# Dilated attention in pairs of blocks, a pair every 24 bulk matmuls, beside the projections of a hybrid decoder layer

## The chip, the cores and the metric

One core of a Trainium2 chip runs the whole program in one launch. The metric is the device time of one execution in microseconds. The kernel before took 2669.09 us (median of 3 runs, 2668.16 to 2672.79).

The engines have names in the profile: PE is TensorE (matmuls and transposes), PEld its weight loads, DVE is VectorE, ACT is ScalarE, POOL is GpSimd, SP is the engine whose queue issues the DMAs. Each engine works through its own list of instructions in a fixed order and waits on semaphores for the others.

## The reference, cut to what matters

One decoder layer for 1024 tokens of width 1024, in float32: a SwiGLU, then a mixer with two branches, then a second SwiGLU, and a last norm. The mixer multiplies the normed tokens by one wide matrix `w_in`. Its first columns give the queries, keys and values of branch A, which is causal attention with dilation: 12 heads of 64 in three groups (dilation 1, 4 and 16). A group regroups the sequence by residue, and a block of 128 queries sees its own block of keys and, in the first two groups, the block before it.

```
s = einsum('brnqhd,brnkhd->brnhqk', qb, kw) * Dh**-0.5
s = where(valid, s, -inf);  m = max(s);  p = exp(s - m);  l = sum(p)
o = einsum('brnhqk,brnkhd->brnqhd', p / l, vw);  lse = m + log(l)
```

The three groups are mixed by a softmax over `lse`. The other columns of `w_in` feed branch B, a gated DeltaNet of 8 heads (short convolution, l2 norm, a triangular solve in every chunk, a scan over the chunks), and the merge gates. `merged @ w_out` is added to the residual.

## The kernel before

The program has a first SwiGLU (to about 750 us), the mixer (to about 1790 us) and the second SwiGLU with the last norm.

In the mixer the projections with `w_in` are the bulk of PE's work: each output tile of 128 x 512 is 24 matmuls in `proj` (line 229: 8 slices of the contraction, three products each, since a float32 operand is split into a high and a low part, H and L). `values` has a shorter bulk matmul for the first group (line 634). Into this stream the class `Weave` puts all the rest. It counts modelled time: `fill` adds 0.23 for a bulk matmul and, when `stretch` has gone by since the last look, polls a heap of tasks (generators) that are due; each polled task records its next few instructions and yields. PE's order is exactly the order of recording (`keep_in_program_order`); on DVE, ACT and SP a list scheduler orders by priority bands (`att` ahead of `h0` ... `h7` ahead of `bulk`) when operands are modelled to be ready.

During attention the stretch is `WIDE`, 2.76, which is 12 bulk matmuls of 0.23; when the last block is done it becomes `STRETCH`, 2.07. I call the instructions of one poll a slot. `attention` (line 789) advances every block that is going by one step in each slot, oldest first, then starts one new block. There are 48 blocks: 3 groups x 2 pairs of heads (`hp`) x 8 blocks. A block needs 256 keys (its own and the block before) or 128. For its two heads, in four slots:

- the scores QK, `tC<-ka` (line 747), one bank of PSUM for each head; head 0 lies in partitions 0 to 63 of the queries and keys, head 1 in 64 to 127. DVE adds the mask and takes the maximum (749), makes `nm` (752), ACT takes the exponential (754);
- an empty step;
- the transposes of the probabilities, `tM<-ident,s` (763), which ACT and DVE copy to `pT` (768, 766);
- the product with the values AV, `tA<-ka,pT` (775); ACT copies it to `o` (777), and a DMA on SP's queue writes `o` to the tensor `od` of the group (786).

So a slot in the middle holds AV of one block, the transposes of a later one, and QK of a third. A float32 matmul that is no transpose appears as two MATMUL records in the profile, a transpose and a bulk matmul (fp32r) as one.

Behind attention come the heads of branch B. For head 0, while attention still runs: the convolutions (927), `products` (L1017 on PE, evicted by DVE at 1019), the blockwise inverse, whose input goes through memory (`nbd`, 1075, and back into the tile `U`, 1079) and which is a chain of small DVE steps (1088, 1089); and turns of 128 x 128 tiles (934), which share the two banks `tA` with AV and the products. Buffers: `ka` has 11 slots of 128 x 1024, `sc` six of 128 x 256, `o` four.

Of the kernel before, what the change touches and what calls it, by code (L numbers as in the profile page):

```python
# [21 lines left out]
NT = T // P  # L22
EPS = 1e-6
NEG = -1.0e30
# [65 lines left out]
def psum(C, tag):  # L90
    return C.pp.tile([P, 512], F32, name=tag, tag=tag, bufs=BANKS[tag])


@contextmanager
def band(C, name):

    saved = C.tc.cur_priority
    C.tc.cur_priority = C.bands[name]
    yield
    C.bands[name] = C.tc.cur_priority  # L100
    C.tc.cur_priority = saved

WIDE, STRETCH = 2.76, 2.07


class Weave:
# [11 lines left out]
    def pe(self, ins, us):  # L120

        self.tc.keep_in_program_order(ins)
        self.now += us
# [24 lines left out]
def in_band(C, name, task):  # L148

    while True:  # L150
        with band(C, name):
            delay = next(task, None)
        if delay is None:
            return
        yield delay
# [6 lines left out]
def t4(C, tag, dt=F32):  # L162
    return C.mx.tile([P, T + {"U": 32, "xp": 16}.get(tag, 0)], dt, name=tag, tag=tag, bufs=TILES[tag])
# [169 lines left out]
def seven_weights(C, w, c0, rest=False):  # L333
# [7 lines left out]
    f1, f2 = raws  # L341
    S = C.fp.tile([P, 4, 4, P], F32, name="wS", tag="wS", bufs=1)
    S1, S2, S3, S4 = [S[:, i] for i in range(4)]
    for out, p, q, op in ((S1, f2[:, 0:4], f2[:, 4:8], ALU.add), (S2, S1, f1[:, 0:4], ALU.subtract),
                          (S3, f1[:, 0:4], f2[:, 0:4], ALU.subtract), (S4, f1[:, 4:8], S2, ALU.subtract)):
        nc.gpsimd.tensor_tensor(out=out, in0=p, in1=q, op=op)  # L346
    W = {}
    for srcs, names, eng in ((f1, (1, 2), nc.vector), (S[:, 0:2].rearrange("p a k n -> p (a k) n"), (5, 6), nc.vector),
                             (S[:, 2:4].rearrange("p a k n -> p (a k) n"), (7, 3), nc.vector), (f2[:, 4:8], (4,), nc.vector)):
        if rest and 1 in names:  # L350
# [291 lines left out]
def decay_cols(C, I):  # L642

    nc = C.nc
    n = NT * HEADS
# [1 line left out]
    def col(name, dt=F32):  # L647
        return C.mx.tile([P, NT, HEADS], dt, name=name)

    pool = t4(C, "g")  # L650
    used = [0]

    def tmp(name, n=NT * HEADS):
        used[0] += n
        v = pool[:, used[0] - n:used[0]]
        return v.rearrange("p (c h) -> p c h", h=HEADS) if name else v
# [7 lines left out]
    e, w, t, u, g = tmp("de"), tmp("dw"), tmp("dt"), tmp("du"), tmp("dg")  # L664
# [32 lines left out]
    ps = psum(C, "tA")  # L697
# [31 lines left out]
    return out  # L729


def attention_block(C, q, k, g, hp, V, b):

    nc = C.nc
    pe = C.weave.pe
    prev = (g == 0 and b > 0) or (g == 1 and b % 2 == 1)
    nk = 256 if prev else P
    mask = C.pair if g == 2 else (C.band if prev else C.band[:, P:])
    k0 = (b - prev) * P
    with band(C, "att"):  # L740
        o = C.mx.tile([P, 132], F32, name="o", tag="o", bufs=4)
        nm = C.mx.tile([P, 2], F32, name="nm", tag="nm", bufs=4)
        S = []
        for h in range(2):
            rows = slice(h * 64, h * 64 + 64)
            ps = psum(C, "tC")
            pe(nc.tensor.matmul(ps[:, :nk], q[rows, b * P:b * P + P], k[rows, k0:k0 + nk], start=True, stop=True), nk * 0.0017)
            s = C.mx.tile([P, 256], F32, name="s", tag="sc", bufs=6)
            nc.vector.tensor_tensor_reduce(s[:, :nk], ps[:, :nk], mask, 1.0, NEG, op0=ALU.add, op1=ALU.max,
                                           accum_out=o[:, 128 + h:129 + h])  # L750
            S.append(s)
        nc.vector.tensor_scalar(nm, o[:, 128:130], -0.125, None, op0=ALU.mult)
        for h in range(2):
            nc.scalar.activation(S[h][:, :nk], S[h][:, :nk], AF.Exp, bias=nm[:, h:h + 1], scale=0.125,
                                 accum_out=o[:, 130 + h:131 + h])
    yield
    yield
    with band(C, "att"):
        pTs = []
        for h in range(2):  # L760
            pt = psum(C, "tM")
            for j in range(nk // P):
                pe(nc.tensor.transpose(pt[:, j * P:j * P + P], S[h][:, j * P:j * P + P], C.ident), 0.11)
            pT = C.mx.tile([P, 256], F32, name="pT", tag="sc", bufs=6)
            if h % 2:
                nc.vector.tensor_copy(pT[:, :nk], pt[:, :nk])
            else:
                nc.scalar.copy(pT[:, :nk], pt[:, :nk])
            pTs.append(pT)
    yield  # L770
    with band(C, "att"):
        po = psum(C, "tA")
        for h in range(2):
            for j in range(nk // P):
                pe(nc.tensor.matmul(po[:, h * 64:h * 64 + 64], pTs[h][:, j * P:j * P + P],  # L775
                                    V[b - prev + j][hp][:, h * 64:h * 64 + 64], start=j == 0, stop=j == nk // P - 1), 0.19)
        nc.scalar.copy(o[:, :P], po[:, :P])
        dst = C.od[g][:, hp, :]
        if g == 0:
            dst = dst[b * P:b * P + P, :]  # L780
        elif g == 1:
            r, n = b // 2, b % 2
            dst = dst.rearrange("(i r) f -> r i f", r=4)[r, n * P:n * P + P, :]
        else:
            dst = dst.rearrange("(i r) f -> r i f", r=8)[b]
        nc.sync.dma_start(dst, o)


def attention(C):

    going = []
    while C.blocks or going or C.more:
        going = [b for b in going if next(b, True) is None]
        if C.blocks and C.blocks[0][0] <= C.weave.now:
            b = C.blocks.pop(0)[1]
            next(b)
            going.append(b)
        yield C.weave.stretch
    C.attended = True
    C.weave.stretch = STRETCH  # L800
# [511 lines left out]
def mixer(C, tc, I):  # L1312

    nc = C.nc
# [5 lines left out]
    gates = [(C_GA + f * P, C.sgad[f]) for f in range(8)] + [(C_GB + f * P, C.sgbd[f]) for f in range(8)]  # L1320

    with tc.tile_pool(name="mx", bufs=1) as C.mx:
        C.logit = C.mx.tile([P, NT, 16], F32, name="logit")
        with band(C, "att"):
            gdn_consts(C, I)
            rope = [t4(C, tag)[:, :T] for tag in ("U", "Tm")]
# [5 lines left out]
        for g in range(3):  # L1332
            V = values(C, I, w_in, g) if g else None
            for hp in range(2):
                q, k = [rope_tile(C, w_in, c0 + g * 256 + hp * P, g) for c0 in (C_QA, C_KA)]
                if V is None:
                    V = values(C, I, w_in, g)
                    for task in (decay_cols, conv_weights):
                        C.weave.add(in_band(C, "att", task(C, I)), 0.5)
                for b in range(NT):  # L1340
                    C.blocks.append((C.weave.now + 10.0, attention_block(C, q, k, g, hp, V, b)))
                    if g == hp == b == 0:
                        C.weave.add(attention(C), 0.0)
        C.heads, C.more, C.segs, C.combining = [], False, False, False
# [30 lines left out]
        while work or gates or last:  # L1375
            if work and free(*work[0]):
                what, h = work.pop(0)
# [265 lines left out]
```

## Time and profile before

| | |
|---|---|
| profiled execution, its own time | 2673.94 us |
| its span, first to last instruction | 2672.2 us |
| median of 3 timed runs | 2669.09 us |
| PE matmul busy | 2581.1 us, 97% of the span |
| DVE, ACT, POOL busy | 55%, 39%, 18% |
| granted TensorE clock, mean | 0.99 |
| first QK starts, last AV starts | 784.58 us, about 1057 us |

Read it so: PE has work in hand nearly all the time, so what it spends per instruction and what it waits for is the time of the kernel. The other engines count where PE waits for them. The stretch that the change touches is 784 to 1057 us, and the beginning of the heads behind it.

### The profile page before, as it was taken

The page shows a single profiled execution, that of the slowest core. Times are in us where ns is not written, and L with a number is a line of the kernel's source. Part 1 is how long each engine was busy: PE and PEld are TensorE (multiplying, and loading weights), DVE is VectorE, ACT ScalarE, POOL GpSimd, SP SyncE. Part 2 cuts the span into 40 slices and gives each one's busy share as a digit, 9 for nine tenths or more (in the row PEclk, how much of TensorE's full clock was granted, in tenths as well). Part 3 has the DMA queues.
Part 4 walks back from the last instruction along what each step waited for, and adds up shares of the span by engine and source line. Part 5 has one row for each costly group of instructions (what it writes and reads, how often), then busy time and mean ns, then how long its engine had stood idle before and what let it go on. Part 6 is the DMA issues. An engine that isn't in the chain of part 4 may idle for free. (4 is left out here: it accounts for less than half of the span.)

```text
span 2672.2 us, 34694 instructions
## 1 busy us (share of the span) xinstructions
PE 2581.1 (97%) x13007; PEld 2138.7 (80%) x13007; DVE 1463.4 (55%) x3276; ACT 1032.2 (39%) x1738; POOL 468.3 (18%) x378
## 2 busy tenths in 40 slices
PE   6999999999999999999999999999999999999997
PEld 5888888788788788787788888877877888887886
DVE  6444444432743547868867878445764444444326
ACT  5333333211544338445454444344433333332113
POOL 5534442000200000000000000000004445430002
PEclk9999999999999999999999999999999999999999
DMA  5323223531331222223222222367533232226311
GB/s 151 90 88 89 81 76 97 199 101 58 112 99 51 74 74 55 62 68 90 78 62 62 60 59 72 121 204 241 182 99 104 79 90 87 80 83 216 102 57 71
DMA packets 298809, 262.12 MB, mean 98 GB/s; under 512 B 39856, under 2 KB 232592, under 8 KB 298640
## 3 DMA queue, kind: packets, MB, share of 16 engines
q1 hardware_dynamic: 298640, 259.90, 31.9%
q8 instruction: 102, 1.67, 0.3%
q14 instruction: 67, 0.55, 0.1%
HBM read 195.26 MB, written 58.29 MB: 95 GB/s over the span
## 5 line engine op out<-in xcount | busy, mean ns | idle before, releaser
L229 PE MATMUL mm<-hH,wL 128*128 128x512 f32 x1072 | 442.0, 412 | 0.1
L229 PE MATMUL mm<-hL,wH 128*128 128x512 f32 x1072 | 419.8, 392 | 0.0
L229 PE MATMUL mm<-hH,wH 128*128 128x512 f32 x1072 | 418.9, 391 | 0.0
L204 ACT CAST wH<-wraw 128x1024 fp32r<-128x1024 f32 (+1 forms) x138 | 143.7, 1045 | 300.8 <-PE mm L537 123.8
L229 PEld LDWEIGHTS mm<-hL,wH 128*128 128x128 f32 x1072 | 201.5, 188 | 45.7
L229 PEld LDWEIGHTS mm<-hH,wL 128*128 128x128 f32 x1072 | 202.2, 189 | 43.7 <-issue 5.3
L205 DVE TENSOR_TENSOR wL<-wraw,wH 128x1024 fp32r<-128x1024 f32 (+1 forms) x138 | 169.7, 1231 | 112.8 <-ACT wH L204 105.6
L229 PEld LDWEIGHTS mm<-hH,wH 128*128 128x128 f32 x1072 | 202.5, 189 | 35.1
L355 DVE TENSOR_TENSOR wL<-wS,wH 128x1024 fp32r<-128x1024 f32 x88 | 126.8, 1441 | 162.1 <-ACT wH L354 161.3
L346 POOL TENSOR_TENSOR wS<-wraw 128x512 f32<-128x512 f32 x66 | 84.1, 1295 | 563.9 <-PE tA L296 322.8
L423 POOL TENSOR_TENSOR su<-su,sg 128x512 f32<-128x512 f32 x84 | 133.3, 1598 | 185.8 <-DVE su L397 161.6
L354 ACT CAST wH<-wS 128x1024 fp32r<-128x1024 f32 x88 | 92.5, 1053 | 151.0 <-PE tC L365 110.0
L393 ACT COPY ev<-mm 128x512 f32<-128x512 f32 (+1 forms) x118 | 68.5, 581 | 201.7 <-PE mm L365 201.7
L537 PE MATMUL mm<-wH,hidH 128*128 128x512 f32 x352 | 137.8, 392 | 3.0 <-DVE x L539 1.9
L537 PE MATMUL mm<-wH,hidL 128*128 128x512 f32 x352 | 137.5, 391 | 2.6 <-DVE hidL L205 2.6
L537 PE MATMUL tC<-wH,hidH 128*128 128x512 f32 x352 | 137.4, 391 | 1.9 <-ACT wH L204 1.9
L537 PE MATMUL mm<-wL,hidH 128*128 128x512 f32 x352 | 137.1, 390 | 1.3 <-DVE wL L205 1.3
L537 PE MATMUL tC<-wL,hidH 128*128 128x512 f32 x352 | 137.6, 391 | 0.5 <-DVE wL L205 0.5
L537 PE MATMUL tC<-wH,hidL 128*128 128x512 f32 x352 | 137.7, 391 | 0.0
L914 POOL MEMSET xp<- 128x3 f32 x24 | 2.4, 100 | 653.9 <-PE tA L775 250.9
L539 DVE SCALAR_TENSOR_TENSOR x<-mm,x 128x512 f32<-128x512 f32 x64 | 44.0, 689 | 105.2 <-PE mm L537 104.3
L539 DVE SCALAR_TENSOR_TENSOR x<-tC,x 128x512 f32<-128x512 f32 x64 | 44.0, 688 | 86.6 <-PE tC L537 86.5
(432 smaller groups left out, 6029.0 us busy)
## 6 DMA issues: line engine op xcount, KB each, us to landing
wraw<-in_w_in_dram SPq DMA_DIRECT2D x64, 512.0 KB, 4.1
wraw<-in_ffn_w_gate_dram SPq DMA_DIRECT2D x48, 512.0 KB, 4.6
hd<-su SPq DMA_DIRECT2D x84, 256.0 KB, 3.2
wraw<-in_ffn_w_down_dram SPq DMA_DIRECT2D x33, 512.0 KB, 4.3
wraw<-hd SPq DMA_DIRECT2D x33, 512.0 KB, 4.7
wraw<-in_ffn_w_up_dram SPq DMA_DIRECT2D x26, 512.0 KB, 4.7
xs<-in_ffn_w_up_dram SPq DMA_DIRECT2D x22, 512.0 KB, 3.9
wraw<-in_w_branch_b_dram SPq DMA_DIRECT2D x16, 512.0 KB, 4.5
```

The source lines that it names most:

```text
L204: nc.scalar.copy(H[:, :width], raw[:, :width])
L205: (nc.gpsimd if C.pool_split else nc.vector).tensor_tensor(out=L[:, :width], in0=raw[:, :width], in1=H[:, :width].bitcast(F32), op=ALU.sub ...
L229: ins = nc.tensor.matmul(ps, w[:, k, :], x[:, k, :], start=k == 0 and i == 0, stop=k == kt - 1 and i == 2)
L346: nc.gpsimd.tensor_tensor(out=out, in0=p, in1=q, op=op)
L354: nc.scalar.copy(H[:, :n], srcs)
L355: eng.tensor_tensor(out=L[:, :n], in0=srcs, in1=H[:, :n].bitcast(F32), op=ALU.subtract)
L393: nc.scalar.copy(v[:, s], ps[:, s])
L423: (eng or C.nc.gpsimd).tensor_tensor(out=out, in0=out, in1=sg, op=ALU.mult)
L537: nc.tensor.matmul(ps, h[:, m], w, start=i == 0, stop=i == len(seq) - 1)
L539: nc.vector.scalar_tensor_tensor(xs, ps, 0.5, xs, op0=ALU.mult, op1=ALU.add)
L914: nc.gpsimd.memset(xp[:, 0:3], 0.0)
```

## The change

`WIDE` becomes 5.52, so a slot comes every 24 bulk matmuls. A task is now a pair of neighbouring blocks, and each of its three steps does both blocks: QK of both (per head, both blocks into one bank at columns 0 and 256), then the transposes of both in the next slot (the empty step is gone), then AV of both into one bank with one copy on ACT. The scores of a pair lie in one `ka` slot; `o` holds two blocks and has three buffers. The logits of the decay move from a tile of their own into the tile `g`.

```
-WIDE, STRETCH = 2.76, 2.07
+WIDE, STRETCH = 5.52, 2.07
...
-def attention_block(C, q, k, g, hp, V, b):
+def attention_pair(C, q, k, g, hp, V, b0):
...
+        o2 = C.mx.tile([P, 2, 132], F32, name="o", tag="o", bufs=3)
+        nm = C.mx.tile([P, 4], F32, name="nm", tag="nm", bufs=4)
+        S2 = t4(C, "ka")[:, :T].rearrange("p (b h n) -> p b h n", b=2, h=2)
+        banks = [psum(C, "tC") for _ in range(2)]
+        for h, ps in enumerate(banks):
+            rows = slice(h * 64, h * 64 + 64)
+            for i, (b, prev, nk) in enumerate(blocks):
+                k0 = (b - prev) * P
+                pe(nc.tensor.matmul(ps[:, i * 256:i * 256 + nk], q[rows, b * P:b * P + P], k[rows, k0:k0 + nk], start=True, stop=True), nk * 0.0017)
+        for i, (b, prev, nk) in enumerate(blocks):
+            mask = C.pair if g == 2 else (C.band if prev else C.band[:, P:])
+            for h, ps in enumerate(banks):
+                nc.vector.tensor_tensor_reduce(S2[:, i, h, :nk], ps[:, i * 256:i * 256 + nk], mask, 1.0, NEG, op0=ALU.add, op1=ALU.max,
+                                               accum_out=o2[:, i, 128 + h:129 + h])
...
-    yield
     yield
...
+        for i, (b, prev, nk) in enumerate(blocks):
             pt = psum(C, "tM")
+            for h in range(2):
+                for j in range(nk // P):
+                    pe(nc.tensor.transpose(pt[:, h * 256 + j * P:h * 256 + j * P + P], S2[:, i, h, j * P:j * P + P], C.ident), 0.11)
...
         po = psum(C, "tA")
...
+        nc.scalar.copy(o2[:, :, :P], po[:, :2 * P].rearrange("p (b n) -> p b n", n=P))
...
-        C.logit = C.mx.tile([P, NT, 16], F32, name="logit")
+        C.work = t4(C, "g")
+        C.logit = C.work[:, D - 16 * NT:].rearrange("p (c n) -> p c n", n=16)
```

On PE, in the middle of the first group, this is a slot before, with the first bulk matmuls behind it (12 stand between this slot and the next):

```order
L229 MATMUL mm<-hL_3515,wH 128x512
L775 MATMUL tA<-ka,pT 128x64 x4
L763 MATMUL tM<-ident,s 128x128 x4
L747 MATMUL tC<-ka 128x256 x2
L229 MATMUL mm<-hH_3514,wL 128x512
```

and this is a slot now, of the second pair of heads (24 bulk matmuls stand between it and the next); its QK is of a first block with 128 keys and a second with 256, so that the order of the four can be seen:

```order
L229 MATMUL mm<-hH_3514,wL 128x512
L782 MATMUL tA<-ka,pT 128x64 x8
L767 MATMUL tM<-ident,ka 128x128 x8
L750 MATMUL tC<-ka 128x128
L750 MATMUL tC<-ka 128x256
L750 MATMUL tC<-ka 128x128
L750 MATMUL tC<-ka 128x256
```

Two slots have become one. In QK both blocks of head 0 now stand ahead of both blocks of head 1, where the two heads took turns before. There are 48 QK batches before and 24 now.

On SP's queue, where the last blocks of attention meet the inverse of head 0, the order was

```order
L786 DMA od_74<-o 128x132 x5
L1075 DMA nbd_108<-ka 32x8x32 x4
L203 DMA wraw<-in_w_in_dram 128x8x128
L1079 DMA U<-nbd_108 32x1024 x2
L786 DMA od_74<-o 128x132
L1079 DMA U<-nbd_108 32x1024 x2
L786 DMA od_74<-o 128x132 x2
```

and is now

```order
L794 DMA od_74<-o 128x132 x6
L203 DMA wraw<-in_w_in_dram 128x8x128
L1083 DMA nbd_108<-ka 32x8x32 x4
L1087 DMA U<-nbd_108 32x1024
L794 DMA od_74<-o 128x132 x2
L1087 DMA U<-nbd_108 32x1024 x3
L203 DMA wraw<-in_w_in_dram 128x8x128
```

Of the four loads of `U`, two stood behind a write of one block, and three now stand behind the writes of a pair.

## Rows read from the trace of the kernel before

**Rows 1.** Page, head.

```profile
span 2672.2 us, 34694 instructions
```

**Rows 2.** Windows: length, busy us of each engine (instructions), clock, DMA share, GB/s.

```profile
784.00:1056.00 272.00, 270.84 (x1493) 217.96 (x1492) 140.51 (x424) 138.75 (x395) 1.67 (x6) 1.00 0.25 65
1056.00:1100.00 44.00, 39.43 (x186) 32.57 (x186) 40.29 (x118) 25.28 (x40) 3.12 (x7) 0.96 0.20 47
```

**Rows 3.** Waits of PE, 780 to 1030 us: us in total, times, longest.

```profile
PE tA L597 <- ACT xp L607: 0.2, 1, 0.2
```

**Rows 4.** Waits of PE, 1030 to 1100 us.

```profile
PE tA L934 <- DVE ka L1019: 3.9, 1, 3.9
PE tA L934 <- ACT Dm L1003: 0.7, 1, 0.7
```

**Rows 5.** Timeline of PE, a slot with 256 keys: start, us, instruction.

```profile
839.92 1.00 PE L775 MATMUL tA<-ka,pT 128*128 128x64 f32 x8
...
841.29 0.70 PE L747 MATMUL tC<-ka 64*128 64x256 f32 x4
...
842.26 0.39 PE L229 MATMUL mm<-hH,wH 128*128 128x512 f32 x1
...
842.73 0.39 PE L229 MATMUL mm<-hH,wL 128*128 128x512 f32 x1
...
844.55 0.39 PE L229 MATMUL mm<-hL,wH 128*128 128x512 f32 x1
```

**Rows 6.** Timeline of PE, sixteen float32 records in a row.

```profile
1125.88 1.95 PE L1061 MATMUL tA<-U,ka 128*128 128x128 f32 x16
1127.66 0.71 PE L1017 MATMUL tA<-ka 128*128 128x128 f32 x4
```

**Rows 7.** Windows, line 747 alone: matmuls in flight in brackets.

```profile
841.28:841.30 0.02, 0.01 (x2) 0.01 (x2) 1.00 0.00 0
...
841.60:841.62 0.02, 0.02 (x4) 0.00 (x0) 1.00 0.00 0
```

**Rows 8.** Timeline of PE, a slot with 128 keys.

```profile
1015.72 0.56 PE L775 MATMUL tA<-ka,pT 128*128 128x64 f32 x4
...
1017.20 0.40 PE L229 MATMUL mm<-hH,wH 128*128 128x512 f32 x1
```

**Rows 9.** Timeline of PEld behind a QK batch.

```profile
841.92 0.19 PEld L229 LDWEIGHTS mm<-hH,wL 128*128 128x128 f32 x1 [0.33 <-issue]
842.03 0.19 PEld L229 LDWEIGHTS mm<-hH,wH 128*128 128x128 f32 x1
```

**Rows 10.** Timeline of PE, a merge step of the inverse.

```profile
1110.81 1.09 PE L1137 MATMUL tM<-Tm,ka 32*32 32x32 f32 x32
1111.83 0.50 PE L229 MATMUL mm<-hH,wL 128*128 128x512 f32 x1
```

**Rows 11.** Windows in that step, line 1137 alone.

```profile
1111.00:1111.10 0.10, 0.10 (x9) 0.10 (x7) 1.00 0.00 0
...
1111.30:1111.40 0.10, 0.10 (x13) 0.10 (x10) 1.00 0.00 0
```

**Rows 12.** Lines by form, 784 to 1056 us: count, busy us, mean ns.

```profile
L747 PE MATMUL tC<-ka 64*128 64x256 f32 x88 | 15.5, 428 | 0.0
...
L747 PE MATMUL tC<-ka 64*128 64x128 f32 x104 | 12.8, 323 | 0.0
```

**Rows 13.** Timeline of DVE, first mask of a block.

```profile
842.11 0.42 DVE L749 CUSTOM_DVE_ANT_0 s<-tC,masks 128x256 f32<-128x256 f32 x1 [0.29 <-PE tC L747]
```

**Rows 14.** Timeline of ACT, last sum of that block.

```profile
844.03 0.19 ACT L754 ACTIVATION_READ_ACCUMULATOR s<-s,nm 128x1 f32 x1
```

**Rows 15.** Timeline of SP's queue, loads of U held by a write.

```profile
1043.02 0.78 SPq L1079 DMA_DIRECT2D U<-nbd  x2
1047.87 0.34 SPq L786 DMA_DIRECT2D od<-o  x1
1048.26 1.84 SPq L1079 DMA_DIRECT2D U<-nbd  x2
```

More of the change, by code (lines that the diff above doesn't have):

```diff
@@ L648, in col @@
         return C.mx.tile([P, NT, HEADS], dt, name=name)
-    pool = t4(C, "g")
+    pool = C.work
     used = [0]
@@ L729, in rope_tile @@
     return out
-def attention_block(C, q, k, g, hp, V, b):
+def attention_pair(C, q, k, g, hp, V, b0):
     nc = C.nc
     pe = C.weave.pe
[L736 to L739, printed above, removed]
+    blocks = []
+    for b in (b0, b0 + 1):
+        prev = (g == 0 and b > 0) or (g == 1 and b % 2 == 1)
+        blocks.append((b, prev, 256 if prev else P))
     with band(C, "att"):
[L741 to L744, printed above, removed]
-            rows = slice(h * 64, h * 64 + 64)
[L746 to L755, printed above, removed]
-    yield
@@ new lines, in attention_pair @@
+        for i, (b, prev, nk) in enumerate(blocks):
[3 more added lines that the diff above has]
+                                               accum_out=o2[:, i, 128 + h:129 + h])
+            nc.vector.tensor_scalar(nm[:, i * 2:i * 2 + 2], o2[:, i, 128:130], -0.125, None, op0=ALU.mult)
+            for h in range(2):
+                nc.scalar.activation(S2[:, i, h, :nk], S2[:, i, h, :nk], AF.Exp, bias=nm[:, i * 2 + h:i * 2 + h + 1], scale=0.125,
+                                     accum_out=o2[:, i, 130 + h:131 + h])
@@ L759, in attention_block @@
         pTs = []
-        for h in range(2):
+        for i, (b, prev, nk) in enumerate(blocks):
             pt = psum(C, "tM")
[L762 to L769, printed above, removed]
+            for h in range(2):
+                for j in range(nk // P):
+                    pe(nc.tensor.transpose(pt[:, h * 256 + j * P:h * 256 + j * P + P], S2[:, i, h, j * P:j * P + P], C.ident), 0.11)
+            for h in range(2):
+                pT = C.mx.tile([P, 256], F32, name="pT", tag="sc", bufs=6)
+                if h % 2:
+                    nc.vector.tensor_copy(pT[:, :nk], pt[:, 256:256 + nk])
+                else:
+                    nc.scalar.copy(pT[:, :nk], pt[:, :nk])
+                pTs.append(pT)
     yield
@@ L772, in attention_block @@
         po = psum(C, "tA")
[L773 to L786, printed above, removed]
+        for i, (b, prev, nk) in enumerate(blocks):
+            for h in range(2):
+                c0 = i * P + h * 64
+                for j in range(nk // P):
+                    pe(nc.tensor.matmul(po[:, c0:c0 + 64], pTs[i * 2 + h][:, j * P:j * P + P],
+                                        V[b - prev + j][hp][:, h * 64:h * 64 + 64], start=j == 0, stop=j == nk // P - 1), 0.19)
+        nc.scalar.copy(o2[:, :, :P], po[:, :2 * P].rearrange("p (b n) -> p b n", n=P))
+        for i, (b, prev, nk) in enumerate(blocks):
+            dst = C.od[g][:, hp, :]
+            if g == 0:
+                dst = dst[b * P:b * P + P, :]
+            elif g == 1:
+                r, n = b // 2, b % 2
+                dst = dst.rearrange("(i r) f -> r i f", r=4)[r, n * P:n * P + P, :]
+            else:
+                dst = dst.rearrange("(i r) f -> r i f", r=8)[b]
+            nc.sync.dma_start(dst, o2[:, i, :])
 def attention(C):
@@ L1339, in mixer @@
                         C.weave.add(in_band(C, "att", task(C, I)), 0.5)
-                for b in range(NT):
-                    C.blocks.append((C.weave.now + 10.0, attention_block(C, q, k, g, hp, V, b)))
+                for b in range(0, NT, 2):
+                    C.blocks.append((C.weave.now + 10.0, attention_pair(C, q, k, g, hp, V, b)))
                     if g == hp == b == 0:
```

## The prediction

> **What bounds the kernel now.** I read the head of the page first, then busy time in windows. The span is 2672.2 us [rows 1], and from 784 to 1056 us, the stretch of attention, PE is busy 270.84 of 272 us at the full clock (1.00, the 2.4 GHz level), while DVE and ACT are at about half [rows 2]. The list of waits says the same: from 780 to 1030 us PE waited 0.2 us in all [rows 3]. So in this stretch only what PE itself spends counts, in useful streaming and in the joints between kinds of work. Just behind it, from 1056 to 1100 us, DVE is busy 40.29 of 44 us [rows 2], and PE waits there 3.9 us for the eviction of a product and 0.7 us for ACT [rows 4]. There another engine's work sets the time. So the change must be priced twice: by PE's joints, and by what it does to those waits.
>
> The timeline of PE prices a joint. In bulk work a matmul starts every 1.82 / 8 = 0.2275 us (842.73 to 844.55, eight steps) [rows 5]. A slot with 256 keys takes from 839.92 to 842.26; one bulk matmul lies in that, so the slot costs 2.34 - 0.23 = 2.11 us. What must stream in it: 8 AV records at 1.78 / 16 = 0.111 each [rows 6], 0.89; 4 transposes, one record each, at the same pace, 0.44; and QK. QK has two records for each head. The windows show two in flight in the first 0.02 us, and the next two from 841.60 on [rows 7]: the heads run side by side, each pair of records for 0.21 us, 256 columns at the 0.111 us that 128 columns take [rows 6]. So QK streams 0.43. Sum 1.76; the joint costs 2.11 - 1.76 = 0.35. The slot with 128 keys gives 1.48 - 0.23 = 1.25 against 0.45 + 0.22 + 0.21 = 0.88, a joint of 0.37 [rows 8]. Both sizes give the same joint, which is what a fixed cost looks like. I take 0.36. It is paid at the change into and out of the half-height matmuls: the first bulk matmul behind QK loads its weights only when QK is over, and the next follows 0.34 us later instead of 0.23 [rows 5, 9].
>
> **The change, part by part.**
>
> Fewer slots. The streaming is the same: the same matmuls of the same sizes, in pairs. 48 QK batches become 24, so 24 joints go: 24 x 0.36 = -8.6 us, all of it on PE's own path. This is the main term; if only the part seen behind QK counted (0.34 - 0.23 and one weight load of 0.11 us [rows 9], so 0.22), it would be -5.3.
>
> The heads side by side. Before, the two records of head 0 stood ahead of those of head 1; now four do. Whether PE still reaches past them is the open price. The nearest rows are those of the inverse's merge (line 1137), 16 records in one row group and 16 in another: 9 are in flight in the steady state, and 13 between 1111.30 and 1111.40 [rows 11]. The 32 records take from 1110.81 to 1111.83, 0.032 us each [rows 10], so the first group's last would start at 1110.81 + 15 x 0.032 = 1111.3. To have four more in flight just then, the second group must have come in some three records before that, while three of the first were still to start. Three are just what now lies between head 0's first record and head 1's first. I therefore expect head 1 to start when head 0's first has its weights and really streams, one weight load later: 0.11 us [rows 9], paid once in each batch: 24 x 0.11 = +2.6 us. Bounds: 0, if they start together as now; and fully one after the other. For the latter: 88 / 4 = 22 blocks with 256 keys and 104 / 4 = 26 with 128 [rows 12] stream 22 x 0.43 + 26 x 0.21 = 14.9 us side by side, and would take as much again, +14.9.
>
> A rule speaks for the bad end. The Trainium skill, "TensorE: Matmul & The Clock Gate", Part 3, Packing small matmuls, says that only weight loads are pulled ahead and that matmuls start and end in strict program order. By that rule nearly all of head 0 would run before head 1, and the sum would be about +4 instead of -8. The trace does not agree: with starts in order the count of line 1137 would stay at 9 throughout, and it rises to 13 [rows 11].
>
> Exponentials, copies, writes. The same four mask steps and four exponentials per pair; the copies of AV halve in number; the 48 writes of `od` stay. All run beside PE, on engines half idle [rows 2]. Their cover is the distance from QK to the transposes. Before, it was two slots of 12 and a full slot between; now 24 bulk matmuls, 24 x 0.2275 = 5.5 us, and the AV records of another pair, up to 16 x 0.111 = 1.8: 7.2 us. One block needs 2.1 us from its first mask to its last sum (842.11 to 844.22) [rows 13, 14]; of the pair the masks of the second block run under the exponentials of the first, so about 1 + 2 x 1.1 = 3.2 us. Four microseconds of slack are left for what else stands in ACT's queue. I price this at 0; at the other end, one microsecond for each of the 8 pairs of the third group, whose exponentials meet the convolutions: +8.
>
> The `ka` slot for the scores, three `o` buffers, logits in `g`: each frees or takes memory. An `o` buffer comes back one whole slot (7 us or more) before the third pair after it writes. 0, with the same +8 as the bound if a tile has to wait.
>
> The end of attention. Here the lists of the engines stand differently. On PE, between the first products of head 0 and the third products, in front of the turn that waited 3.9 us, 159 bulk matmuls stood before and 168 stand now: 9 x 0.2275 = 2.0 us more of PE's own work before it gets there. The work itself is moved, not added. DVE's chain to that eviction hangs on the loads of `U`, and those on SP's queue: before, two loads lay behind a write of `od` that waited from 1043.8 to 1047.87 for AV [rows 15]; now three lie behind the writes of the pair. That AV stands about as far behind the products as before: 1.78 for their 16 records, 24 bulk matmuls 5.5, a turn 0.44 and the second products 1.78, together 9.5 us; before 1.78 + a slot of 1.25 + 12 bulk matmuls 2.7 + 0.44 + 1.78 = 8.0, and what PE waited between. So I take it that DVE is there as early as before and PE 2.0 us later: of the 4.6 us of waits [rows 4] 2.0 go. Bounds: -4.6, all of it; and +4, if the loads come later by as much as they were held (4.1 us).
>
> Behind 1100 us the order shifts by a few bulk matmuls here and there; waits of one to three microseconds will move in both directions. 0.
>
> Sum: -8.6 + 2.6 - 2.0 = -8.0. The profiled execution of 2673.94 us (span 2672.2, 1.7 around it) would become 2665.9. It was 4.9 above the median of the runs, 2669.09; on that median the forecast is **2661 us**.
>
> **The rivals.**
>
> Serial heads. One mechanism, in the 24 QK batches: head 1 waits until head 0's four records are through. Price +14.9 instead of +2.6: -8.6 + 14.9 - 2.0 = +4.3, 2673 us, slower than before. It decides as soon as the delay in a batch is over (8.6 + 2.0) / 24 = 0.44 us. For it: the order on PE, and that nothing in attention itself shows a reach over three records. Against it: the rise to 13 in flight [rows 11].
>
> The waits come back. The transposes wait for the exponentials, or the heads behind attention lose as much as the joints gave: 4 to 8 us, so 2665 to 2669 us. For it: DVE's 92% in 1056 to 1100 us, and that all of a pair's work arrives at once. Against it: 0.2 us of waits in the whole stretch of attention [rows 3].
>
> More than forecast. Heads start together (0 instead of +2.6), and all 4.6 us of waits go: 2656 us. For it: QK before started both heads within 0.02 us [rows 7].
>
> **How the numbers follow.** Forecast 0.62, with its own range 2657 to 2665 from half a skew either way and the waits behind 1100 us; waits back 0.16; more than forecast 0.12; serial heads 0.10. The range 2655 to 2670 us leaves out the serial case and the far edge of the best. About 0.2% (5.3 us) is what the timed runs can tell from no change. Faster by more than that: 0.12 and nine tenths of 0.62, 0.68. Within: the rest of the forecast, 0.06, and the returning waits, 0.16, so 0.22. Slower: 0.10.
>
> **What would show it.** In the trace after, 24 slots with QK, each costing 2 x 1.76 + 0.36 + 0.11 = 4.0 us for two blocks with 256 keys, where two slots cost 4.2; the second head's first QK record about 0.1 us behind the first's; PE's waits to 1030 us still under 1.5 us; and the wait for the third products' eviction near 2 us. The forecast is wrong if a QK batch of 256 columns takes over 1.5 us from its first record to the first bulk matmul (0.63 before [rows 5, 9], 1.2 expected), if transposes wait for ACT in more than a few slots, or if the waits behind 1056 us grow by more than 4.

## The result, and the profile after

The changed kernel took 2656.1 us (median), and its ratio to the kernel before was 0.9942, 95% interval [0.9926, 0.9957]. Two more comparisons of the same two kernels gave 0.9927 [0.9914, 0.9939] and 0.9954 [0.9941, 0.9968]. So it is 12 to 20 us faster, about 15; the forecast was 8 (2661 us, ratio 0.9970), outside all three intervals. The stated range of 2655 to 2670 us begins at a ratio of 0.9947: two of the three ratios lie below it.

Head of the page after, which answers to [rows 1]:

```profile
span 2657.2 us, 34573 instructions
```

Windows of after over the stretches of [rows 2]: length, busy us of PE, PEld, DVE, ACT and POOL (instructions), clock, DMA share, GB/s.

```profile
784.00:1056.00 272.00, 271.54 (x1537) 225.73 (x1536) 141.72 (x439) 138.29 (x382) 1.77 (x7) 1.00 0.26 69
1056.00:1100.00 44.00, 42.24 (x230) 35.06 (x229) 39.16 (x122) 24.53 (x45) 4.49 (x6) 1.00 0.26 62
```

In the stretch of attention PE is as full as before and does more in it (1537 records instead of 1493). In the 44 us behind it PE is busy 2.8 us more, and its clock is 1.00 where it was 0.96. Of the waits of PE from 1030 to 1100 us [rows 4] one is left:

```profile
PE tA L942 <- DVE ka L1027: 1.8, 1, 1.8
```

A slot of after on PE's timeline, to be laid beside [rows 5]: start, us, instruction.

```profile
834.94 1.90 PE L782 MATMUL tA<-ka,pT 128*128 128x64 f32 x16
836.67 0.82 PE L767 MATMUL tM<-ident,ka 128*128 128x128 f32 x6
837.42 1.14 PE L750 MATMUL tC<-ka 64*128 64x256 f32 x8
838.49 0.50 PE L229 MATMUL mm<-hH,wH 128*128 128x512 f32 x1
838.83 0.39 PE L229 MATMUL mm<-hL,wH 128*128 128x512 f32 x1
```

From its first record to the second bulk matmul behind it are 838.83 - 834.94 = 3.89 us, less one bulk matmul 3.66. Its records stream 16 x 0.111 + 6 x 0.111 + 0.86 = 3.31. The joint is 0.35: a slot of a pair pays what a slot of one block paid.

To place the rest I numbered the bulk matmuls in order of start in both traces and compared the time from one number to another. The work between two numbers is nearly the same in all kernels of the table, so the differences are joints, waits (PE idle, in brackets) and clock. Attention is 3300 to 4112. In 4112 to 4260 lie the third products of head 0 (the third of its batches of 16 records in `products`); the turn behind them waits for DVE's eviction, and I call this the wait at the third products. Behind them come the later heads.

| kernel | 3300 to 4112 | 4112 to 4260 | 4260 to 5400 |
|---|---|---|---|
| before | 277.3 (1.2) | 45.6 (4.6) | 384.0 (12.3) |
| before, a second trace | 277.3 (1.2) | 45.7 (4.6) | 385.4 (10.8) |
| after | 267.9 (0.5) | 41.5 (1.8) | 382.5 (8.9) |
| after, a second trace | 267.9 (0.5) | 41.5 (1.8) | 382.4 (8.7) |
| after, a third trace | 267.9 (0.5) | 41.5 (1.8) | 383.8 (9.9) |

So -9.4 in attention, -4.1 at the third products, -1.5 in the later heads: -15.0, which is the difference of the spans, since the parts in front and behind (+1.3 and -1.2) nearly cancel. The first two differences come out the same in the other traces; the third lies anywhere between -0.2 and -3.0, by the pair of traces that is taken.

Of the -4.1, 2.8 are waits. The rest lies near what the low clock cost before. First the turn of before that waited and the windows around its wait of 3.9 us, then the windows of after around its 1.8 us:

```profile
1092.40 1.09 PE L934 MATMUL tA<-ident,ka 128*128 128x128 f32 x4 [3.92 <-DVE ka L1019]
```

```profile
1086.00:1090.00 4.00, 2.48 (x20) 2.17 (x18) 3.97 (x12) 0.85 (x2) 0.10 (x1) 1.00 0.44 82
1090.00:1094.00 4.00, 1.60 (x6) 1.54 (x7) 3.92 (x8) 0.77 (x2) 0.40 (x1) 0.76 0.49 114
1094.00:1100.00 6.00, 6.00 (x24) 4.81 (x24) 4.53 (x9) 1.72 (x3) 0.00 (x0) 0.87 0.13 22
```

```profile
1078.00:1084.00 6.00, 4.24 (x30) 3.76 (x29) 5.62 (x26) 0.20 (x2) 0.95 (x1) 1.00 0.02 5
1084.00:1100.00 16.00, 16.00 (x99) 13.11 (x98) 12.31 (x28) 8.47 (x17) 1.47 (x1) 1.00 0.43 93
```

Before, the granted clock fell to the 1.2 GHz level at the end of the wait: 4 x 0.24 = 0.96 us short of full clock in the second window is 1.9 us at half clock, so it fell at 1092.1 us, and PE went on at 1092.40. The two windows are 4 x 0.24 + 6 x 0.13 = 1.7 us short; less what fell into the wait itself, about 1.6 us were lost by it. With the 2.8 of waits that is 4.4, 0.3 more than the difference, which I can't place. After, with half the wait, the clock stays at 1.00.

### The profile page after: what moved, and what is told of

Same layout as the page of the kernel before. It is cut to its first block, busy times and chain, and to the rows that moved or that the text cites. A ratio compares the mean times of both kernels' runs of the same rounds, so it can differ in the third digit from the quotient of the medians.

```text
span 2657.2 us, 34573 instructions
## 1 busy us (share of the span) xinstructions
PE 2574.7 (97%) x13007; PEld 2140.1 (81%) x13007; DVE 1459.2 (55%) x3276; ACT 1017.2 (38%) x1706; POOL 469.6 (18%) x378
## 5 line engine op out<-in xcount | busy, mean ns | idle before, releaser
L229 PE MATMUL mm<-hH,wH 128*128 128x512 f32 x1072 | 438.4, 409 | 0.0
L229 PE MATMUL mm<-hH,wL 128*128 128x512 f32 x1072 | 419.6, 391 | 0.1
L229 PEld LDWEIGHTS mm<-hH,wL 128*128 128x128 f32 x1072 | 201.4, 188 | 45.5 <-DVE wL L205 0.5
```

The lines of the kernel that those rows point to most:

```text
L229: ins = nc.tensor.matmul(ps, w[:, k, :], x[:, k, :], start=k == 0 and i == 0, stop=k == kt - 1 and i == 2)
```

## The experiments

**The trace of before again**, without an edit.

> The kernel before once more, unaltered, for its trace: theory (the 3.9 us wait at the third products and the low clock behind it belong to the kernel and not to one execution): a wait of 3.5 to 4.3 us there again, the clock at its lower level for some 3 us behind it, and bulk 4112 to 5400 in 428 to 431 us. Rival (they vary from run to run): a wait under 2.5 us.

Waits of PE, 1030 to 1100 us:

```profile
PE tA L934 <- DVE ka L1019: 3.9, 1, 3.9
PE tA L1017 <- DVE ka L1019: 1.0, 1, 1.0
```

The wait is the same, the clock fell to its lower level at 1092.9 us, and 4112 to 5400 took 431.1 us. It belongs to the kernel. The same for the changed kernel:

> The changed kernel once more, unaltered, to see what of its gain stays from one execution to the next. Theory (the gain is the joints, about -9 us in attention, plus some 6 us of waits that go because the head work stands at other places): PE idle between the third products and bulk matmul 4800 is again near 5.7 us against 12.1 us before, and the ratio again near 0.994. Rival (the excess over the forecast is the variation of one profiled execution): that idle time comes out anywhere between 5 and 12 us, and the ratio nearer 0.997.

Ratio 0.9927; its row stands in the table. And once more, beside the last variant:

> The changed kernel, for comparison on the same chip: ratio 0.9927 to 0.9942, as it came out before.

0.9954; the third trace in the table. The ratio moves by more than one interval says, and so do the later heads (1.4 us); the first two stretches in the table don't.

**Both heads in turns.** The order of the four QK matmuls is changed, nothing else.

```
-        for h, ps in enumerate(banks):
-            for i, (b, prev, nk) in enumerate(blocks):
+        for i, (b, prev, nk) in enumerate(blocks):
+            for h, ps in enumerate(banks):
```

> The changed kernel with the four QK matmuls of a pair in turns of the heads (head 0, head 1, head 0, head 1) instead of both of head 0 first. Theory (PE reaches past all four records of head 0 anyway): nothing changes, bulk 3300 to 4112 takes 267.9 us within 0.3, and a batch with 256 keys in both blocks 1.41 us from its first record to the second bulk matmul. Rival (one weight load of skew hidden in each batch): 2.6 us less, 265.3, and 1.3 us a batch.

Attention took 268.1 us, a batch with 256 keys 1.402 us (1.408 in the changed kernel); ratio 0.9952 [0.9938, 0.9966]. The order of the heads costs nothing here, so no skew is there to be taken back. In the trace of the changed kernel head 1's first record starts 0.013 us behind head 0's (0.007 before).

**More records of head 0 ahead.** Does PE reach as far as one likes?

```
-                pe(nc.tensor.matmul(ps[:, i * 256:i * 256 + nk], ...), nk * 0.0017)
+                for n0 in range(0, nk, 128): pe(nc.tensor.matmul(ps[:, i * 256 + n0:i * 256 + n0 + 128], ...), 128 * 0.0017)
```

> The changed kernel with each 256-key QK matmul cut into two of 128 keys: for a pair with 256 keys in both blocks 8 records of head 0 now stand ahead of the first of head 1, 4 where both have 128. Theory (PE starts the other row group however many records of the first stand ahead): both heads start within 0.02 us and the batch stays near 1.41 us to the second bulk matmul. Rival (PE reaches past four records at most): head 1 starts 0.2 to 0.45 us behind head 0, and the batch takes 1.6 to 1.9 us.

Neither. Windows of line 750 alone, matmuls in flight in brackets; first the changed kernel at the start of a batch with 4 records of head 0 ahead, then this one with 8, at the start of the batch and when the other head joins:

```profile
837.42:837.44 0.02, 0.02 (x2) 1.00 0.00 0
```

```profile
836.64:836.66 0.02, 0.02 (x1) 1.00 0.00 0
...
837.20:837.29 0.09, 0.09 (x4) 1.00 0.00 0
```

The records of that batch start 0, 0.213, 0.325, 0.437, 0.548 and 0.554 us behind the first, then two by two. The sixth is head 1's first: it starts 0.006 us behind the fifth of head 0, when three of head 0 are still to start. With 6 ahead it starts 0.006 us behind the third, again with three to go; with 4, behind the first. So with 4, 6 or 8 records ahead PE starts the other row group as soon as only three of the first are left, and what stands ahead beyond that is serial: a batch took 1.974 us with 8 ahead instead of 1.408, 1.528 with 6 instead of 1.202, 0.989 with 4, as in the changed kernel. There are 6 and 10 such batches: 6 x 0.566 + 10 x 0.326 = 6.7; attention took 274.1 us, 6.2 more. A pair of blocks is just the size that goes for nothing.

The Trainium skill, "TensorE: Matmul & The Clock Gate", Part 3, Packing small matmuls, says that matmuls start and end in strict program order. These starts disagree. Two records of one row group never start less than 0.1 us apart here; the sixth starts 0.006 us behind the fifth, so it is head 1's, and by program order three records of head 0 stand in front of it. The trace has a second sign of this: only the last record of a head signals DVE, and the first signal in the batch comes with the record at 0.883 us, the eleventh; if the first eight were all head 0's, it would come with the eighth.

**QK in two slots.** Pairs as they are, but the QK of the two blocks 12 bulk matmuls apart; a slot every 12, a new pair in every second. The loop over the two blocks now stands around QK, masks and exponentials, with a yield at its end.

```
-WIDE, STRETCH = 5.52, 2.07
+WIDE, STRETCH = 2.76, 2.07
...
+    for i, (b, prev, nk) in enumerate(blocks):
+        with band(C, "att"):
...
+        yield
...
+        turn = not turn
-        if C.blocks and C.blocks[0][0] <= C.weave.now:
+        if turn and C.blocks and C.blocks[0][0] <= C.weave.now:
```

> Pairs as in the changed kernel (one tile for the scores, transposes and AV of both blocks together), but QK of the two blocks in two slots 12 bulk matmuls apart: 48 QK batches again. Theory (a joint of 0.36 us for each QK batch): bulk 3300 to 4112 takes 8 to 9 us more than in the changed kernel, about 276 us. Rival (what was saved are the slots with AV and transposes, or the copies): under 271 us. The later heads are at places of their own here, so the total can differ by some us either way; expected ratio 0.997 (0.994 to 1.001).

Attention took 300.3 us, 32 more than the changed kernel, of which PE idled 16.8; ratio 1.0066 [1.0045, 1.0087]. I laid the waits to the `o` buffers and tried again with AV one slot earlier.

> Once more QK of the two blocks of a pair in two slots 12 bulk matmuls apart, but AV one slot earlier, so that an `o` buffer is held no longer than in the changed kernel; there the masks waited for `o` when AV came later. Theory (0.36 us for each QK batch; the 16.8 us of PE waits of the first try came from the `o` buffers): PE idles under 3 us from bulk 3300 to 4112, and the stretch takes 276 to 278 us against 268. Rival (splitting a pair costs more than the joints, by the places of transposes and masks): PE busy there beyond 278 us, or waits for the masks again. Total about 0.9970, with the head work near the changed kernel's places.

The same: 299.8 us (14.2 idle), ratio 1.0090 [1.0073, 1.0107]. That theory fell. Waits of PE, 780 to 1030 us, and then the timeline of DVE in front of the first of the four:

```profile
PE tC L752 <- DVE o L753: 10.9, 4, 3.2
```

```profile
794.83 0.42 DVE L771 COPY pT<-tM 128x256 f32<-128x256 f32 x1 [0.25 <-ACT pT L773]
795.17 0.68 DVE L724 TENSOR_TENSOR xp<-xp,U 128x512 f32<-128x512 f32 x1
795.77 0.68 DVE L725 TENSOR_TENSOR vb<-vb,Tm 128x512 f32<-128x512 f32 x1
796.49 0.69 DVE L728 TENSOR_TENSOR ka<-xp,vb 128x512 f32<-128x512 f32 x1
797.10 0.42 DVE L753 CUSTOM_DVE_ANT_0 ka<-tC,masks 128x256 f32<-128x256 f32 x1
```

The masks that free the two banks of QK stand on DVE behind copies and behind the rotation of the next queries and keys. With QK every 24 matmuls that is late by nothing; with QK every 12, PE stands. And again the clock follows. Windows around that wait:

```profile
790.00:797.00 7.00, 4.39 (x23) 3.19 (x22) 2.42 (x5) 1.52 (x5) 0.00 (x0) 0.97 0.16 37
797.00:803.00 6.00, 5.42 (x13) 3.98 (x14) 2.24 (x12) 3.71 (x10) 0.00 (x0) 0.50 0.01 2
803.00:810.00 7.00, 7.00 (x43) 5.81 (x42) 3.90 (x9) 1.80 (x6) 0.00 (x0) 0.97 0.38 93
```

Over attention the low clock cost up to 8.5 us (17.1 us at half clock). 299.8 - 267.9 = 31.9 are 13.7 of waits, 8.5 of clock, and 9.7, where 24 more joints ask for 8.6. The total proves little; the joint is better read slot by slot (below).

**QK together, AV apart.** A slot every 12 again; transposes and QK of a pair in one, AV alone in the next.

```
-WIDE, STRETCH = 5.52, 2.07
+WIDE, STRETCH = 2.76, 2.07
...
+    yield
     yield
     with band(C, "att"):
         pTs = []
...
+        turn = not turn
-        if C.blocks and C.blocks[0][0] <= C.weave.now:
+        if turn and C.blocks and C.blocks[0][0] <= C.weave.now:
```

> QK of a pair still in one batch (24 batches), but a slot every 12 bulk matmuls: transposes and QK in every second slot, AV alone in the slots between. The head work behind attention stands at the same places on PE as in the kernel before. Theory (the joint belongs to the half-height QK batch, and the excess of the gain comes from the places of the head work): bulk 3300 to 4112 takes 268 us as in the changed kernel (277 before), but PE idles about 12 us again from there to bulk 4800, so the time is about 9 us under before, ratio 0.9965. Rival 1 (a joint is paid at every change between attention and bulk): the stretch takes about 276 us again and the ratio is near 0.9995. Rival 2 (the places of the head work do not matter): as fast as the changed kernel, 0.994.

Ratio 0.9969 [0.9957, 0.9982], as the theory had it, though the parts are less neat. A slot of AV alone on PE:

```profile
846.52 1.90 PE L783 MATMUL tA<-ka,pT 128*128 128x64 f32 x16
848.22 0.48 PE L229 MATMUL mm<-hH,wL 128*128 128x512 f32 x1
848.54 0.39 PE L229 MATMUL mm<-hH,wH 128*128 128x512 f32 x1
```

848.54 - 846.52 - 0.23 = 1.79 us for 16 records that stream 1.78: full-height float32 work has no joint. Counted so, a slot with QK cost 0.34 to 0.35 us over its streaming in before and in after, with 4 records of QK or 8; AV alone 0.01 to 0.02; AV and transposes -0.05. The joint belongs to the QK batch, and rival 1 is out. But attention took 272.4 us, not 268: 1.4 us of waits, and 3 beside them. About 1 of these stands in the slots themselves: transposes and QK without AV in front cost 0.36 to 0.40 us here, where the changed kernel's slots cost 0.34 to 0.35. The other 2 I can't place. At the third products (45.5) PE waited as before:

```profile
PE tA L944 <- DVE ka L1029: 3.5, 1, 3.5
PE tA L944 <- ACT Dm L1013: 0.5, 1, 0.5
```

**Other tasks every 12 matmuls.** Pairs every 24, but polls of all else every 12.

```
-WIDE, STRETCH = 5.52, 2.07
+WIDE, STRETCH = 2.76, 2.07
...
-        yield C.weave.stretch
+        yield 2 * C.weave.stretch
```

> Pairs every 24 bulk matmuls as in the changed kernel, but all other tasks are polled every 12 again. The first and second products then stand where they stood before (12 bulk matmuls apart), the later heads where the changed kernel has them. Theory (places of the head work make the excess): attention as in the changed kernel, 268 us for bulk 3300 to 4112; the waits at the third products near 2 to 3 us; those of the later heads as in the changed kernel, so a ratio of 0.994 to 0.995. Rival (the coarser polling during attention is what removed the waits): PE idles 10 to 12 us from bulk 4112 to 4800, ratio 0.9965.

Attention 269.6 us (2.3 idle, the transposes wait three times for exponentials), 4112 to 4260 43.5 (2.1), ratio 0.9923 [0.9911, 0.9936], beside 0.9927 of the changed kernel in the same comparison. So it shows no need for the coarser polls. The wait at the third products is only 0.3 us longer than in the changed kernel (2.1 and 1.8), but here the clock fell behind it:

```profile
1085.00:1089.00 4.00, 4.00 (x13) 3.17 (x12) 4.00 (x6) 2.02 (x3) 0.00 (x0) 0.57 0.00 0
```

4 x 0.43 = 1.7 us, which with the 0.3 is the whole difference of 2.0 to the changed kernel's 41.5. So where a wait of about two microseconds remains, as in the changed kernel, the clock's part of the gain is not safe.

**The places of the head work.** First the kernel before with one more wide slot behind the last block, which moves the third products by 3 bulk matmuls.

```
     yield C.weave.stretch
+    yield C.weave.stretch
     C.attended = True
```

(the added line stands behind the loop of `attention`)

> The kernel before, single blocks and 48 QK batches, with nothing changed but that the wide stretch lasts one slot longer at the end of attention, which moves the head work behind it by some bulk matmuls: third products 3 later, fourth products of head 1 and all that follows 6 to 12 later or earlier, near the places that the variant with pairs and 12-matmul polls has. Theory (those places, not the pairs, take the waits away behind attention): bulk 3300 to 4112 takes 277 us as before, and bulk 4112 to 5400 takes 424 to 427 us against 429.6 before; ratio about 0.998. Rival (the pairs themselves relieve ACT, DVE or the queue): 429 to 430 us again, ratio 1.000.

Ratio 1.0007 [0.9996, 1.0019]; 46.5 and 383.6 us. No gain: this place is not the changed kernel's. Then the exact places, in both directions. The polls behind attention come every 9 matmuls, so their phase can be set by one poll, 1.61 (7 matmuls) behind the last step in the kernel before, 0.46 (2) in the changed one:

```
+    C.weave.stretch = 1.61
+    yield C.weave.stretch
     C.attended = True
     C.weave.stretch = STRETCH
```

> The kernel before, single blocks and 48 QK batches, with one more poll 7 bulk matmuls (1.61) behind the last step of attention: from the third products of head 0 on, the head work stands on PE at the very bulk matmuls where the changed kernel has it (third products at 3878 instead of 3871 by the order, fourth 3977, then 4215, 4462, 4489). Theory (these places make the gain behind attention): bulk 3300 to 4112 in 277 us as before, the wait at the third products near 2 us instead of 3.9, no low clock behind it, and bulk 4112 to 5400 in 424 to 426 us against 430 to 431; ratio 0.998. Rival (the pairs relieve DVE, ACT or the queue): 430 us or more, ratio 1.000.

> The changed kernel with one more poll 2 bulk matmuls (0.46) behind the last step of attention: from the third products of head 0 on, the head work stands where the kernel before has it (3871, 3979, 4226, 4455, 4500). Theory (places): bulk 3300 to 4112 in 268 us, the wait at the third products 3.5 us or more with low clock behind it, and bulk 4112 to 5400 in 429 to 430 us; ratio 0.9960 to 0.9965, nearly the forecast. Rival (the pairs): 424 us and a ratio of 0.993 to 0.994.

Ratios 0.9984 [0.9975, 0.9993] and 0.9943 [0.9926, 0.9960]. The places alone are worth 4 us to the kernel before; taking them from the changed kernel costs it nothing that can be seen. For the stretch of the first, its trace was taken again:

> The kernel before with the head work at the changed kernel's places once more, for its trace. From its time (0.9984 of before, 4 us less) and from the run that gave the changed kernel the old places (third products' wait still 1.8 us, 4112 to 5400 in 425 us): if the places made the 4 us, bulk 4112 to 5400 takes about 426 us here and the wait at the third products is under 2.5 us; if the pairs did, the wait stays at 3.5 us or more and the gain, if any, lies behind 1100 us.

| kernel | 3300 to 4112 | 4112 to 4260 | 4260 to 5400 |
|---|---|---|---|
| before, new places | 277.2 (1.2) | 42.1 (2.6) | 384.1 (10.3) |
| after, old places | 267.9 (0.5) | 41.6 (1.8) | 383.5 (12.0) |

Waits of PE from 1030 to 1100 us, of the first and of the second:

```profile
PE tA L936 <- DVE ka L1021: 2.6, 1, 2.6
PE tA L1019 <- DVE ka L1021: 1.0, 1, 1.0
```

```profile
PE tA L944 <- DVE fsT L1099: 1.8, 1, 1.8
```

Attention doesn't care for the places, nor do the later heads taken together. At the third products either is enough: with PE 7 matmuls (1.6 us) later the wait is 2.6 us instead of 3.9, with the pairs 1.8, and in both traces the clock stays up. The two don't add.

What the pairs do there can be read from DVE. Its waits from 1030 to 1091 us, before and after:

```profile
DVE vb L1181 <- PE tA L934: 2.9, 1, 2.9
...
DVE vT L927 <- ACT vT L925: 1.3, 1, 1.3
```

```profile
DVE pT L771 <- ACT pT L773: 2.0, 3, 1.5
...
DVE vb L1189 <- PE tA L942: 0.3, 1, 0.3
```

Before, DVE stood 2.9 us for a turn that PE made late, in a stretch that DVE itself bounds; after, 0.3. That is enough for the two microseconds, but other waits of DVE moved too, and the variant with AV apart, without that wait, still had 3.5 us on PE. The kernel before at the new places still has DVE's 2.9 us, so its gain there is PE's later place alone. Which DVE wait decides stays open.

**Two ideas on that wait.** The writes of `od` from ACT's queue, so that no load of `U` stands behind them:

```
-            nc.sync.dma_start(dst, o2[:, i, :])
+            nc.scalar.dma_start(dst, o2[:, i, :])
```

> The changed kernel with the od writes issued from ACT's queue instead of SP's, so that no load of U stands behind a write of a pair. Theory (the hold of U, 2.4 us on SP's queue from 1038.3 to 1040.7 us, delays DVE's chain to the third products' eviction): all U loads go out within 1.5 us, and the wait of 1.8 us there falls below 0.5. Rival (DVE's own throughput sets it, as the run with AV in a slot of its own suggests, where U was not held and PE waited 3.5 us): the wait stays between 1.2 and 2.5 us.

SP's queue, changed kernel and then this one:

```profile
1037.98 0.31 SPq L1087 DMA_DIRECT2D U<-nbd  x1
1040.70 0.83 SPq L794 DMA_DIRECT2D od<-o  x2
1041.57 1.74 SPq L1087 DMA_DIRECT2D U<-nbd  x3
```

```profile
1032.08 1.71 SPq L1087 DMA_DIRECT2D U<-nbd  x4
```

The hold is gone and the wait is 1.6 us instead of 1.8. The queue on which I hung DVE's chain does not set it. It is one execution, 2655.4 us, and attention took 2.5 us more there (270.4, of which 2.6 idle). Then the weight splits on POOL:

```
-        C.heads, C.more, C.segs, C.combining = [], False, False, False
+        C.heads, C.more, C.segs, C.combining, C.pool_split = [], False, False, False, True
```

> The changed kernel with the weight splits wL (1.22 us each on DVE, 40 of them between 1100 and 1740 us) on POOL instead, from the end of attention to the end of the mixer. Theory (the waits behind attention hang on how much work stands on DVE in front of an eviction): the wait at the third products goes from 1.8 us to under 0.5, bulk 4112 to 5400 takes 418 to 421 us against 424, and the ratio becomes about 0.992. Rival (POOL needs twice as long, about 2.6 us for a split by its 1.3 us for half the size, and the weights come late, or it slows DVE): new waits of the bulk matmuls for wL, ratio 0.995 or more.

Ratio 1.0093 [1.0063, 1.0124]; the wait grew to 2.3 us and the later heads took 402.0 us. In fact the splits go to POOL from 963 us on, before the end of attention, which took 271.9 us. A split takes twice as long on POOL (count, busy us, mean ns):

```profile
L205 POOL TENSOR_TENSOR wL<-wraw,wH 128x1024 fp32r<-128x1024 f32 x44 | 106.1, 2410 | 402.7 <-ACT wH L204 343.6 <-PE tC L1237 30.3 <-PE tC L1247 12.6
```

And a step of DVE that begins inside a split is held until the split ends. On DVE and on POOL, start and us:

```profile
1073.46 0.20 DVE L1096 TENSOR_TENSOR fsP<-fsT,U 128x40 f32<-128x40 f32 x1
...
1074.18 1.85 DVE L1097 TENSOR_TENSOR fsT<-fsT,fsP 128x40 f32<-128x40 f32 x1
```

```profile
1073.57 2.40 POOL L205 TENSOR_TENSOR wL<-wraw,wH 128x1024 fp32r<-128x1024 f32 x1 [2.65 <-ACT wH L204]
```

The step of 1.85 us ends at 1076.03, the split at 1075.97. Of 16 such steps between 1050 and 1790 us, 13 took 0.19 to 0.20 us, as all 16 do in the changed kernel, and three 1.85 to 2.36 us. Over that time 34 steps of DVE were held, some 60 us in all.

The Trainium skill, "SBUF — State Buffer", section "SBUF: two separate sides", says that a DVE operation with two inputs in SBUF and a POOL operation that reads SBUF take a shared pair of ports in turn, each for its whole instruction. The 1.85 us agree.

**QK at the head of the slot.**

```
-        going = [b for b in going if next(b, True) is None]
+        new = []
         if C.blocks and C.blocks[0][0] <= C.weave.now:
...
+        going = [b for b in going if next(b, True) is None] + new
```

> The changed kernel with QK at the head of the slot, in front of AV and the transposes, so that no bulk matmul follows QK at once. Theory (the joint is that full-height weights can be loaded only when the half-height QK is over, whatever follows): the slot costs the same, bulk 3300 to 4112 takes 268 us within 1. Rival (the joint is between float32 work and the bulk's number format, or belongs to the bulk matmul behind QK): it becomes 3 to 8 us shorter or longer.

Attention 268.6 us with 2.1 of waits (0.5 in the changed kernel); ratio 0.9950 [0.9936, 0.9963]. A slot cost 0.24 to 0.26 us over its streaming instead of 0.34 to 0.35. The slot with the same records as the changed kernel's at 834.94:

```profile
835.23 1.14 PE L750 MATMUL tC<-ka 64*128 64x256 f32 x8
836.30 2.00 PE L782 MATMUL tA<-ka,pT 128*128 128x64 f32 x16
...
839.03 0.39 PE L229 MATMUL mm<-hL,wH 128*128 128x512 f32 x1
```

839.03 - 835.23 - 0.23 = 3.57 us, where the changed kernel took 3.66. So a part of the joint, 0.09, lies between the transposes and QK, and the theory that the place doesn't matter was wrong by that. The rest belongs to QK itself: where it stands alone between bulk matmuls, in the changed kernel,

```profile
889.58 0.93 PE L750 MATMUL tC<-ka 64*128 64x128 f32 x8
...
890.78 0.39 PE L229 MATMUL mm<-hL,wH 128*128 128x512 f32 x1
```

it took 890.78 - 889.58 - 0.23 = 0.97 us for 0.67 of streaming, 0.30 over it. Most of what the new order saved went into the waits. Joined with the polls every 12 matmuls:

> The two variants that cost nothing, together: QK at the head of the slot, in front of AV (there a slot cost 0.24 us over its streaming where the changed kernel's costs 0.34), and all other tasks polled every 12 bulk matmuls. Theory (the joint has a part in front of QK, 0.09 us behind a transpose, that goes when QK follows a bulk matmul and AV follows QK): a slot costs 0.24 again, and if the waits of the changed order (2.1 us there) stay under 1 us, bulk 3300 to 4112 takes 266 us against 268; 1.5 to 2.5 us faster than the changed kernel in the same comparison. Rival (the waits eat it): 268 to 270 us and no difference.

The slot cost 0.24 again, but PE waited 3.8 us in attention and the clock fell behind the longest of these waits (2.6 us), which cost 3.4 us: 273.4 us, ratio 0.9961 [0.9947, 0.9975] beside 0.9954 of the changed kernel. No version was faster than the changed kernel by more than the noise.

## Why the prediction was right or wrong

**Joints, -8.6.** Right. Attention gained 9.4 us, 0.7 of them waits; 8.7 are PE's own; 24 times the joint read from a slot, 0.34 to 0.35, is 8.2 to 8.4. The joint per slot is the same for one block and for a pair, and it goes with the QK batches and not with slots: AV alone has none.

**Heads side by side, +2.6.** Wrong: 2.3 of the 7 us by which the trace's -15.0 went past the sum of -8.0. The reach was right: three records of head 0 may still be to start, as the count at line 1137 said [rows 11], and 6 and 8 records ahead show it. The step that failed is that head 1 would start when head 0's first "has its weights and really streams, one weight load later". It starts 0.013 us behind it, 24 x 0.013 = 0.3 us in all. The serial rival had its mechanism: past three it is paid, 0.566 us a batch at 8 records. A pair stays just under it.

**Exponentials, copies, writes, buffers, 0.** Right for the change: PE waited for none of them in attention. The other bound was not idle: QK every 12 matmuls, or QK first, brought 2 to 17 us of waits.

**The end of attention, -2.0.** The direction was right, the size -4.1. The waits shrank by 2.8, not 2.0, and about 1.6 of low clock behind them went as well. That clock stood in the row itself (0.96 in [rows 2]), and the sum did not use it. "DVE is there as early as before" was wrong: PE's later place explains 1.3 us of the wait by itself (3.9 to 2.6), and the pairs, with PE at its old place, bring it to 1.8. That DVE's chain to the eviction hangs on the loads of `U` [rows 15] did not hold either: with no load held behind a write the wait was still 1.6.

**Behind 1100 us, 0.** Right: -1.5 us, where the two traces of before lie 1.4 apart and so do those of after.

Of the rivals "more than forecast" was the one that came: -8.6 for the joints and all of the 4.6 us were its terms, the second reached by another way (2.8 of waits and 1.6 of clock). That its 2656 us is what was measured is therefore partly luck: a wait of 1.8 us stayed, and the clock, which no term had, made up for it. It had a chance of 0.12, although what spoke for it, two heads within 0.02 us [rows 7], was a direct look at the thing priced and +2.6 was an inference from another line.

## What to carry to other kernels

Where PE has work in hand all the time, count the joints: how often a stretch changes into half-height matmuls, times the joint read from one slot. When two row groups are to run side by side, put no more records of one ahead of the other than the trace shows PE to reach over (here one to start with and three past it). And price a wait of PE together with the clock behind it, in the windows that follow: two microseconds less of waiting can be four.

## What the hardware showed that I had not expected

- A second row group starts 0.006 to 0.013 us behind the record of the first after which three are left, with 4, 6 or 8 recorded ahead.
- The joint is not between number formats: AV and transposes (float32) beside bulk matmuls (fp32r) cost 0.02 us or less. QK behind AV and transposes and before bulk costs 0.34 to 0.35 us, QK alone between bulk matmuls 0.30 to 0.32, QK between bulk and AV 0.24 to 0.26.
- The fourteen longest waits of PE between 780 and 1800 us in these traces (3.2 to 4.5 us) each had the 1.2 GHz level in their last part or right behind them, which cost up to 1.7 or 3.4 us. Shorter ones sometimes had: in the changed kernel one of 1.7 us at 1524 us did, the 1.8 us at the third products did not.
- A DVE step that began inside one of POOL's splits of 2.4 us took until the split was over, 1.85 to 2.36 us instead of 0.20.
